# A modulation bank computed beside the keys and values, and the state-space constants cut into more steps

## The chip, the cores and the metric

The kernel runs on one core of one Trainium2 chip. The metric is the device time of one launch in microseconds, as the median of several runs. TensorE (PE) does matrix products, VectorE (DVE), ScalarE (ACT) and GpSimd (POOL) do the elementwise work, and the queue of SyncE (SP) issues almost all DMAs. Each engine takes its instructions in the order in which the program lists them.

## The reference, cut to what matters

Two layers work on 1152 tokens (1024 latent, 128 context) of width 1024. Layer 0 is windowed attention and a squared-ReLU MLP, layer 1 a state-space mixer (S5) with a GLU and a second MLP. Every block is modulated by vectors that come from a small product with a large weight.

```python
def _modulation(cvec, w_mod, b_mod):
    return jnp.split(jax.nn.silu(cvec) @ w_mod + b_mod, N_MOD, axis=-1)
...
    dt = jnp.exp(log_dt.astype(jnp.float32))[:, None]
    mag = jnp.exp(lam_re * dt)
    ang = lam_im * dt
    ab_re = mag * jnp.cos(ang)
    ab_im = mag * jnp.sin(ang)
...
for i in range(DEPTH):
    sh1, sc1, g1, sh2, sc2, g2 = _modulation(c, w_mod[i], b_mod[i])
    h = _modulate(x, norm1_g[i], sh1, sc1)
    x = x + g1 * mixer(h)            # attention in layer 0, S5 in layer 1
    x = x + g2 * _mlp(_modulate(x, norm2_g[i], sh2, sc2), mlp_w1[i], mlp_w2[i])
```

The S5 mixer needs per-group constants (exponentials, sines, cosines and complex powers of the transition) that depend on weights alone.

## The kernel before, in words

Tokens stand in three chunks of 384 columns. Most products are taken in three passes of a split operand (high by high, low by high, high by low), one matmul per pass, at L45, L46 and L47. The written program is not the final order: a scheduler places instructions on each engine by their place in the code, by priorities and by what they need; from then on each engine keeps that order.

**Start and prologue.** `start` computes modulation bank 0 of layer 0. `attention` then normalizes the chunks in the order 1, 2, 0 and computes keys (`k_part`, PSUM tiles `kps`) and values (`v_part`, `vps`) for each, and at chunk 0 the first two query tiles (`q_items`, `qps`, then `q_put`). The query weights `wq` share two buffers with the key weights `wk`.

**A modulation bank.** `mod_bank(..., ahead=True)` has eight steps. A step multiplies the 1 MB of weights of one k-tile (two tiles `wm` of 512 KB, in the two buffers with tag `wo`) into a PSUM tile `modps` (L163), and only then issues the loads of the next k-tile on SP (L145). In layer 0, two steps share one PSUM tile from a pool of two buffers (tag `st`, which `nps`, `nrb` and `qps` use as well); the sum goes to `modsb`, and four transposes (`modpt`, L178) turn it. The matmuls carry a high priority and are placed no earlier than the last product recorded before them. A generator yields after each step, so that a caller can spread the steps.

**Attention.** 72 units (24 pairs of heads in three blocks each) go through scores (`sps`, L369), softmax on DVE, ACT and POOL, transposes (`tps`), and the product with V (`pvps`). During the first 12 units `modfill` feeds banks 1 and 2 in between (20 yields); from unit 12 on the output projection (`wops`) fills that place. `wops` takes its weights through the `wo` buffers too, and its result needs the gate from bank 1.

**First MLP with the S5 preparation beside it.** `mlp(0, background)` runs 16 blocks of hidden columns. In a block PE does six tiles of the first product (24 matmuls each, called first-layer tiles here), then 24 tiles of the second (6 matmuls each), whose results DVE adds to `x` (L470); PSUM holds six such tiles. `fill` takes 2 steps of the generator `background` after each chunk of the first product and 3 after each chunk of the second:

```python
            def fill(where):
                with self.tc.high_priority(offset=-self.LOW):
                    for _ in range((self.F0, self.F1)[where]):
                        next(gen, None)
```

`background` runs `s5_prep`: 32 small blocks, each with DVE work on the tiles `bb`, `g` and `d`, POOL work on `bm`, a small product `kp` (L1288, reads `g`, high priority) and transposes `bmt`, and every eighth block first `s5_consts`. That one is about 160 short DVE instructions in tiles `ww`, `w2`, `w3` and `pq`, with three yields: after the sines and cosines, after the division, and at the end.

Of the kernel before, what the change touches and what calls it, by code (L numbers as in the profile page):

```python
# [33 lines left out]
class Body:  # L34
# [448 lines left out]
    def attention(self):  # L483
        nc, tc, a = self.nc, self.tc, self.a
        with ExitStack() as ctx:
# [9 lines left out]
            with ExitStack() as c2:  # L495
                P = c2.enter_context(tc.tile_pool(name="pro", bufs=1, reuse_waits="tile"))
                ps = c2.enter_context(tc.tile_pool(name="props", bufs=6, space=PSUM))
                wv = [P.tile([128, 2048], F32R, name=f"wv{i}") for i in range(2)]
                hs = {1: self.h_big(self.H, "h")}
                for _ in self.norm_apply(1, 0, 0, hs[1]):  # L500
                    pass
                nc.sync.dma_start(self.x[2], a["x"][2])
                self.w_kv(1, wv)
                mk = P.tile([128, 2, 128], F32, name="mkf")
                kc = P.tile([128, 2, 128], F32, name="kc")
                nc.sync.dma_start(mk, a["mask"])
                nc.sync.dma_start(self.sink, a["sink"])
                nc.sync.dma_start(kc, a["cache_k"])
                nc.sync.dma_start(self.V[:, 9], a["cache_v"])
                for _ in self.norm_stats(2):  # L510
                    pass
                hs[2] = self.h_small("h2")
                for _ in self.norm_apply(2, 0, 0, hs[2]):
                    pass
                for _ in self.norm_stats(0):
                    pass
                for c in (1, 2, 0):
                    if c == self.CC:
                        nc.vector.tensor_copy(self.mask, mk)
                        nc.vector.tensor_copy(self.identb, self.ident)  # L520
                        nc.vector.tensor_scalar(self.nsink, self.sink, -1.0, None, op0=ALU.mult)
                        for m in range(2):
                            self.put_k(m, kc[:, m, :], 1152, 128)
                    if c == 2:
                        hs[0] = self.h_big(self.H, "h")
                        for _ in self.norm_apply(0, 0, 0, hs[0]):
                            pass
                    tab = self.rope_tab(c)
                    for m in range(2):
                        self.k_part(c, m, hs[c], self.wk, tab, ps)  # L530
                    if c == 0:
                        for t in range(2):
                            out = []
                            for _ in self.q_items(t, hs[0], out):
                                pass
                            Q[t] = self.q_put(out[0], tab)
                    for j in range(3):
                        self.v_part(c, j, hs[c], wv, ps)

            B = ctx.enter_context(tc.tile_pool(name="att2", bufs=2, reuse_waits="tile"))  # L540
            self.B = B
# [36 lines left out]
            stats = {}  # L578

            def modfill():  # L580
                for b in (1, 2):
                    yield from self.mod_bank(0, b, self.R, "wo", 2, 2, B, "modsb", 2, True)

            def pace(r, n, total):

                return (r + 1) * total // n - r * total // n

            fill = modfill()
            nfill = 20
            for i in range(NU):  # L590
                c, t, jj = units[i]
                tau = 8 * c + t
                if jj == 0:
# [5 lines left out]
                    if t == 4:  # L599
                        fill, nfill = self.wo_items(c, 0, otl[c]), 16  # L600
                    if t == 0 and c > 0:
                        fill, nfill = self.wo_items(c - 1, 1, otl[c - 1]), 16
# [462 lines left out]
    def sincos(self, x, s, c, t, z, n):  # L1065

        v = self.nc.vector
        mg = 12582912.0
        self.reduce(x, n, 4)
        v.tensor_tensor(out=z, in0=x, in1=x, op=ALU.mult)  # L1070
        v.tensor_scalar(t, z, -1.9515295891e-4, 8.3321608736e-3, op0=ALU.mult, op1=ALU.add)
        v.tensor_scalar(c, z, 2.443315711809948e-5, -1.388731625493765e-3, op0=ALU.mult, op1=ALU.add)
# [4 lines left out]
        v.scalar_tensor_tensor(out=s, in0=t, scalar=1.0, in1=x, op0=ALU.add, op1=ALU.mult)  # L1077
        v.scalar_tensor_tensor(out=c, in0=c, scalar=-0.5, in1=z, op0=ALU.add, op1=ALU.mult)
        v.tensor_scalar(c, c, 1.0, None, op0=ALU.add)

        v.tensor_scalar(t, n, 0.25, mg, op0=ALU.mult, op1=ALU.add)
        v.tensor_scalar(t, t, mg, None, op0=ALU.subtract)
# [7 lines left out]
        v.tensor_tensor(out=c, in0=c, in1=z, op=ALU.mult)  # L1090
        v.tensor_tensor(out=s, in0=s, in1=t, op=ALU.subtract)
        v.tensor_tensor(out=c, in0=c, in1=x, op=ALU.add)

    NPA = 92
    NT = 147
# [2 lines left out]
    def s5_consts(self, pa, qs):  # L1098
# [6 lines left out]
        an, tt, zz, nn = (w2[:, i] for i in range(4))  # L1105
        sn, cs = (w3[:, i] for i in range(2))
# [3 lines left out]
        s0 = self.s0[:, :, qs]  # L1110
        mag = w[:, 0, :]
        self.exp_dve(dt, dt, w[:, 1, :], w[:, 2, :], w[:, 3, :])

        v.tensor_tensor(out=an[:, 0, :], in0=li, in1=dt, op=ALU.mult)
        v.tensor_tensor(out=w[:, 4, :], in0=lr, in1=dt, op=ALU.mult)
        self.reduce(an[:, 0, :], w[:, 5, :])
        for k in range(7):
            v.tensor_scalar(an[:, k + 1, :], an[:, 0, :], 8.0 * 2.0 ** k, None, op0=ALU.mult)
        self.sincos(an, sn, cs, tt, zz, nn)
        self.exp_dve(w[:, 4, :], mag, w[:, 1, :], w[:, 2, :], w[:, 3, :])  # L1120
        t, q = an[:, 0:8, :], w2[:, 1:3, 0:8, :]
        yield
# [5 lines left out]
        for n in (1, 2, 4):  # L1128
            o = slice(n + 1, 2 * n + 1)
            b = lambda z: z[:, n:n + 1, :].to_broadcast([128, n, G])  # L1130
            self.cmul(v, pr[:, o, :], pi[:, o, :], pr[:, 1:n + 1, :], pi[:, 1:n + 1, :], b(pr), b(pi),
                      t[:, 0:n, :])

        den, rd, nr, fr, fi, t1 = (w[:, 5 + i, :] for i in range(6))
        v.tensor_tensor(out=den, in0=lr, in1=lr, op=ALU.mult)
# [35 lines left out]
        for k in range(4):  # L1171
            n = 1 << k
            m = min(n, 11 - n)
            o = f0 + n
            b = lambda z: (cs, sn)[z][:, k + 1:k + 2, :].to_broadcast([128, m, G])
            self.cmul(v, F_r[:, o:o + m, :], F_i[:, o:o + m, :], F_r[:, f0:f0 + m, :], F_i[:, f0:f0 + m, :],
                      b(0), b(1), t[:, 0:m, :])
        p0, p1 = q[:, 0, 0:2], q[:, 1, 0:2]
        self.cmul(v, p0, p1, cs[:, 5:7, :], sn[:, 5:7, :], cs[:, 3:5, :], sn[:, 3:5, :], t[:, 0:2, :])
        self.cmul(v, E_r[:, 4:6, :], E_i[:, 4:6, :], p0, p1, cs[:, 1:3, :], sn[:, 1:3, :], t[:, 0:2, :])  # L1180
# [6 lines left out]
        for z_r, z_i, n in ((F_r, F_i, f0), (E_r, E_i, e0)):  # L1187
            nc.scalar.copy(z_r[:, 0:n, :], z_r[:, 2 * n:n:-1, :])
            nc.scalar.mul(z_i[:, 0:n, :], z_i[:, 2 * n:n:-1, :], -1.0)

        zs = self.zs[:, qs]
        r8 = zs[:, :, 2]
# [27 lines left out]
    def s5_prep(self, mods):  # L1220
# [9 lines left out]
        for b in range(64 // GB):  # L1230
# [71 lines left out]
                                  bass.AP(tensor=w.tensor, offset=w.offset, ap=[list(w.ap[0]), [16, 8], [1, 128]]))  # L1302
            nc.sync.dma_start(self.ex_d[lo, gs], g[lo, :, :, 1:9, :])
            nc.sync.dma_start(self.ex_d[hi, gs], g[hi, :, :, 0:8, :])
            yield
            bt = M.tile([128, GB, 2, 128], F32, name="bt", tag="bt")
            tp = self.bank("bmt")
            for q in range(GB):
# [410 lines left out]
```

## Time and profile before

| what | value |
|---|---|
| median of 3 runs | 2742.19 us |
| lowest, highest | 2741.9, 2745.39 us |
| profiled execution, its time | 2745.59 us |
| its span, first to last instruction | 2743.5 us |
| mean granted TensorE clock | 0.977 |
| PE busy | 2570.7 us, 94% |
| DVE busy | 1972.1 us, 72% |
| ACT busy | 1220.4 us, 44% |

The profiled execution is one execution, 3.4 us above the median of the others; sums are made against it. A busy PE is counted from the start of a matmul to its modelled end, at whatever clock was granted, so a stretch at half clock looks as busy as one at full clock.

### The profile page before, as it was taken

What the parts mean: (1) busy time and instruction counts of PE and PEld (TensorE: products, weight loads), DVE (VectorE), ACT (ScalarE), POOL (GpSimd) and SP (SyncE); (2) the same over time, 40 slices, a digit from 0 to 9 for tenths busy, and PEclk for the clock granted to TensorE, in tenths of its full rate; (3) what the DMA queues carried; (4) which work ended last, traced back from release to release, by engine and by line L of the source; (5) the groups of instructions that cost most, each with busy time, mean ns of one, the idle gap of its engine ahead of it and who ended that gap; (6) DMA issues with size and microseconds to landing.
All of it is one profiled execution on the core that took longest, in us unless ns stands there. A gap on an engine that the chain in (4) does not pass through costs nothing. (4 is left out here: it accounts for less than half of the span.)

```text
span 2743.5 us, 43899 instructions
## 1 busy us (share of the span) xinstructions
PE 2570.7 (94%) x16369; PEld 2418.0 (88%) x16369; DVE 1972.1 (72%) x4609; ACT 1220.4 (44%) x2519; POOL 366.6 (13%) x492
## 2 busy tenths in 40 slices
PE   6888999999999999999999678999999999999997
PEld 4767898889998998998999666899999999999997
DVE  4845777789778777769764799555577677777677
ACT  3454666665333233323233655443455445434344
POOL 1122322220221221211210310000011001000001
PEclk8999999999999999999999899999999999999998
DMA  7253222222342343343321576433333312111212
GB/s 269 81 164 126 77 82 73 85 74 86 116 134 87 115 130 107 117 123 116 112 91 49 163 234 204 138 123 123 108 121 127 130 66 91 68 62 67 72 63 77
DMA packets 138244, 305.22 MB, mean 111 GB/s; under 512 B 14384, under 2 KB 70064, under 8 KB 136624
## 3 DMA queue, kind: packets, MB, share of 16 engines
q1 hardware_dynamic: 138032, 302.42, 33.8%
q8 instruction: 130, 2.13, 0.3%
q14 instruction: 82, 0.67, 0.1%
HBM read 247.78 MB, written 39.81 MB: 105 GB/s over the span
## 5 line engine op out<-in xcount | busy, mean ns | idle before, releaser
L45 PE MATMUL m<-at,w 128*128 128x384 f32 x1536 | 522.7, 340 | 4.2 <-DVE x L470 1.9
L470 DVE SCALAR_TENSOR_TENSOR x<-m,mod,x 128x384 f32<-128x384 f32 (+2 forms) x1024 | 486.8, 509 | 54.8 <-PE m L47 51.7
L46 PE MATMUL m<-at,w 128*128 128x384 f32 x1536 | 518.6, 338 | 0.2 <-DVE at L879 0.2
L47 PE MATMUL m<-at,w 128*128 128x384 f32 x1536 | 518.5, 338 | 0.0
L45 PEld LDWEIGHTS m<-at,w 128*128 128x128 f32 x1536 | 289.8, 189 | 12.6 <-DVE x L470 5.3
L46 PEld LDWEIGHTS m<-at,w 128*128 128x128 f32 x1536 | 289.4, 188 | 0.7 <-DVE at L879 0.5
L47 PEld LDWEIGHTS m<-at,w 128*128 128x128 f32 x1536 | 289.3, 188 | 0.6 <-issue 0.4
L51 ACT CAST w<-wr 128x1024 fp32r<-128x1024 f32 x160 | 165.8, 1046 | 259.1 <-PE m L46 194.3
L52 DVE TENSOR_TENSOR w<-wr,w 128x1024 fp32r<-128x1024 f32 x160 | 197.4, 1241 | 62.3 <-ACT w L51 55.9
L45 PE MATMUL m<-h,w 128*128 128x384 f32 x512 | 175.1, 342 | 2.3 <-ACT w L51 1.5
L47 PE MATMUL m<-h,w 128*128 128x384 f32 x512 | 174.1, 340 | 2.9 <-DVE w L52 2.7
L45 PE MATMUL m<-mh,w 128*128 128x384 f32 x512 | 176.2, 345 | 0.0
L46 PE MATMUL m<-mh,w 128*128 128x384 f32 x512 | 174.3, 341 | 0.0
L47 PE MATMUL m<-mh,w 128*128 128x384 f32 x512 | 174.2, 341 | 0.0
L46 PE MATMUL m<-h,w 128*128 128x384 f32 x512 | 173.6, 339 | 0.0
L404 POOL TENSOR_SCALAR pt<-pt,sst 128x512 f32<-128x512 f32 (+1 forms) x144 | 103.6, 732 | 304.5 <-DVE sst L402 134.8
L392 ACT ACTIVATE pt<-sps,sst 128x512 f32<-128x512 f32 (+1 forms) x144 | 89.4, 626 | 71.7 <-DVE sst L381 71.4
L784 PE MATMUL m<-hs,ws 128*128 128x384 f32 x576 | 114.4, 338 | 0.0
L697 ACT ACTIVATE r<-m 128x384 f32<-128x384 f32 x96 | 46.9, 490 | 151.5 <-PE m L47 151.3
L52 DVE TENSOR_TENSOR at<-r,at 128x384 fp32r<-128x384 f32 x96 | 55.7, 581 | 76.0 <-ACT at L51 75.8
L380 DVE TENSOR_REDUCE sst<-sps 128x1 f32<-128x512 f32 (+1 forms) x144 | 86.9, 612 | 32.1 <-PE sps L378 29.2
L369 PE MATMUL sps<-K,q 128*128 128x256 f32 (+1 forms) x544 | 96.8, 304 | 11.6 <-DMA q<-q 4.5
(372 smaller groups left out, 5953.9 us busy)
## 6 DMA issues: line engine op xcount, KB each, us to landing
wr<-in_w_dram SPq DMA_DIRECT2D x192, 512.0 KB, 3.8
wm<-in_w_mod_dram SPq DMA_DIRECT2D x80, 512.0 KB, 4.8
wr<-in_glu_dram SPq DMA_DIRECT2D x48, 512.0 KB, 3.2
wr<-in_w_qo_dram SPq DMA_DIRECT2D x24, 512.0 KB, 3.2
wr<-in_w_qo_dram SPq DMA_DIRECT2D x48, 256.0 KB, 2.6
bt<-bt_d SPq DMA_DIRECT2D x16, 768.0 KB, 5.7
dt_d<-d SPq DMA_DIRECT2D x32, 294.0 KB, 3.5
D<-dt_d SPq DMA_DIRECT2D x16, 588.0 KB, 4.7
```

The costliest lines, as they stand in the source:

```text
L45: mm(out, lh, rh, start=first, stop=False)
L46: mm(out, lh, rl, start=False, stop=False)
L47: self.mm = mm(out, ll, rh, start=False, stop=last)
L51: (ceng.copy if ceng is self.nc.scalar else ceng.tensor_copy)(h, src)
L52: seng.tensor_tensor(out=l, in0=src, in1=h, op=ALU.subtract)
L369: nc.tensor.matmul(ps[:, 128 * i0:128 * i0 + w], lhs, rhs, start=(part == 0 and i0 == 0), stop=part == 1 and n == 8)
L380: nc.vector.tensor_reduce(out=mx[:, e:e + 1], in_=ps[:, :nk], axis=AX.X, op=ALU.max)
L392: nc.scalar.activation(p[:, e, :nk], sps[e][:, :nk], AF.Exp, scale=SCALE, bias=ng[:, e:e + 1], accum_out=sm[:, e:e + 1])
L404: nc.gpsimd.tensor_scalar(p[:, e, :nk], p[:, e, :nk], rc[:, e:e + 1], 1.0, op0=ALU.mult, op1=ALU.mult)
L470: nc.vector.scalar_tensor_tensor(out=self.x[c][:, m, lo:hi], in0=ps[:, lo:hi], scalar=self.gate(layer, j, m, s), in1=self.x[c][:, m, lo:hi ...
L697: nc.scalar.activation(r, pt[:, :CW], AF.Relu)
L784: self.nc.tensor.matmul(p[:, :CW], w[i][:, x, j, :], B[i][j][y], start=f and k == 0, stop=j == 3 and k == 2, skip_group_check=True)
```

## The change

Bank 1 of layer 0 is taken out of `modfill` and becomes a generator of its own, `early`, made before the loop over the chunks and advanced by one after each key part and after the first two value parts: twelve places for its ten yields. `modfill` keeps bank 2, and its pace is set for 10 instead of 20 yields over the same 12 units. In `s5_consts` the three yields become fourteen (thirteen cuts inside the work and one at its end); the arithmetic stays the same. In `s5_prep` the yield between the stores of a block and its transposes goes, so that a block takes five steps instead of six.

```diff
+                early = self.mod_bank(0, 1, self.R, "wo", 2, 2, P, "modsb", 2, True)
                 for c in (1, 2, 0):
...
                     for m in range(2):
                         self.k_part(c, m, hs[c], self.wk, tab, ps)
+                        next(early, None)
...
                     for j in range(3):
                         self.v_part(c, j, hs[c], wv, ps)
+                        if j < 2:
+                            next(early, None)
+                for _ in early:
+                    pass
...
             def modfill():
-                for b in (1, 2):
-                    yield from self.mod_bank(0, b, self.R, "wo", 2, 2, B, "modsb", 2, True)
+                yield from self.mod_bank(0, 2, self.R, "wo", 2, 2, B, "modsb", 2, True)
...
-            nfill = 20
+            nfill = 10
...
     def sincos(self, x, s, c, t, z, n):
         self.reduce(x, n, 4)
+        yield
...
         v.tensor_scalar(c, c, 1.0, None, op0=ALU.add)
+        yield
...
         v.tensor_tensor(out=c, in0=c, in1=x, op=ALU.add)
+        yield
...
         self.exp_dve(dt, dt, w[:, 1, :], w[:, 2, :], w[:, 3, :])
+        yield
...
-        self.sincos(an, sn, cs, tt, zz, nn)
+        yield
+        yield from self.sincos(an, sn, cs, tt, zz, nn)
...
         for n in (1, 2, 4):
...
             self.cmul(v, pr[:, o, :], pi[:, o, :], pr[:, 1:n + 1, :], pi[:, 1:n + 1, :], b(pr), b(pi),
                       t[:, 0:n, :])
+            yield
...
         for k in range(4):
...
+            if k % 2:
+                yield
...
             nc.scalar.mul(z_i[:, 0:n, :], z_i[:, 2 * n:n:-1, :], -1.0)
+        yield
...
             nc.sync.dma_start(self.ex_d[hi, gs], g[hi, :, :, 0:8, :])
-            yield
             bt = M.tile([128, GB, 2, 128], F32, name="bt", tag="bt")
```

The built programs show where the scheduler puts the moved work. Three places matter.

**The end of the prologue on PE.** Before, these rows stand just ahead of the first scores: one step of bank 1 among the matmuls of the third query tile.

```order
L46 MATMUL qps<-h,wq 128x384
L47 MATMUL qps<-h,wq 128x384
L163 MATMUL modps<-wm,csil 32x512 x4
L45 MATMUL qps<-h,wq 128x384
L46 MATMUL qps<-h,wq 128x384
```

Now the last three steps of bank 1 stand at the end of the values of chunk 0, with its transposes behind them, and only then the first query tile.

```order
L45 MATMUL vps<-wv_237,h 128x256
L46 MATMUL vps<-wv_238,h 128x256
L163 MATMUL modps<-wm,csil 32x512 x4
L47 MATMUL vps<-wv_237,h 128x256
L45 MATMUL vps<-wv_237,h 128x256
L46 MATMUL vps<-wv_238,h 128x256
L47 MATMUL vps<-wv_237,h 128x256
L163 MATMUL modps<-wm,csil 32x512 x8
L178 MATMUL modpt<-ident,modsb 128x128 x4
L45 MATMUL qps<-h,wq 128x384
L46 MATMUL qps<-h,wq 128x384
```

All eight steps of bank 1 now precede the queries; the first of them stands among the transposes `nrb` of the last norm statistics of the prologue (L238), and four matmuls of V are all that stands between the sixth and the seventh.

**The first small product after the second set of constants, on PE and DVE.** Before, PE has `kp_9892` inside the second product's tile `m2_9935`:

```order
L47 MATMUL m2_9927<-at_9530,w2_9372 128x384
L45 MATMUL m2_9935<-at_9530,w2_9371 128x384
L46 MATMUL m2_9935<-at_9530,w2_9371 128x384
L1288 MATMUL kp_9892<-g_9874,bz_9780 32x128 x8
L47 MATMUL m2_9935<-at_9530,w2_9372 128x384
```

and DVE finishes `g_9874` (its last row is L1034) among the constants in `ww`, just ahead of the addition of tile `m2_9911`, which PE computes three tiles before `m2_9935`:

```order
L1032 TENSOR_TENSOR ww_9460<-pq_7303 64x16 x2
L1200 TENSOR_TENSOR ww_9460<-ww_9460 128x16
L1037 TENSOR_TENSOR ww_9460<-ww_9460 64x16 x2
L1034 SCALAR_TENSOR_TENSOR g_9874<-g_9874,t_9875 128x2x144
L1201 TENSOR_TENSOR ww_9460<-ww_9460 128x16
L470 SCALAR_TENSOR_TENSOR x1_71<-m2_9911,mod0_93,x1_71 128x384
```

Now DVE finishes the corresponding `g_10203` among the first-layer splits `at_9936` of the next block (L1040 is the same line as L1034 before),

```order
L1043 TENSOR_TENSOR ww_9582<-ww_9582 64x16
L52 TENSOR_TENSOR at_9936<-r_9992,at_9936 128x384
L1043 TENSOR_TENSOR ww_9582<-ww_9582 64x16
L1040 SCALAR_TENSOR_TENSOR g_10203<-g_10203,t_10204 128x2x144
L1216 TENSOR_TENSOR ww_9582<-ww_9582 128x16
```

and PE has the product that reads it eight tiles into that block's second product, behind the tiles that use `at_9936`:

```order
L46 MATMUL m2_10277<-at_9936,w2_9926 128x384
L47 MATMUL m2_10277<-at_9936,w2_9927 128x384
L1303 MATMUL kp_10295<-g_10203,bz_10122 32x128 x8
L163 MATMUL modps_8248<-wm_9517,csil_73 32x512 x2
L163 MATMUL modps_8248<-wm_9515,csil_73 32x512 x2
```

The distance from `g` to `kp` grows from a few second-product tiles to the rest of the first product and eight tiles.

**The third set of constants on DVE.** Before, its rows around the splits of block 8 (counting from 0) are mostly its end, mixed with the next small block's `g` and `d`:

```order
L1032 TENSOR_TENSOR ww_11672<-pq_7303 64x16
L1200 TENSOR_TENSOR ww_11672<-ww_11672 128x16
L52 TENSOR_TENSOR at_12164<-r_12190,at_12164 128x384
L1037 TENSOR_TENSOR ww_11672<-ww_11672 64x16
L1296 SCALAR_TENSOR_TENSOR ks_12053<-eye_89,dcol_90,ks_12053 64x16
```

Now nearly the whole set stands in the first product of block 8, from the exponential on:

```order
L1058 SCALAR_TENSOR_TENSOR ww_11808<-ww_11808 128x16
L52 TENSOR_TENSOR at_11847<-r_11873,at_11847 128x384
L1079 TENSOR_SCALAR w3_11807<-w2_11806 128x128
L1084 SCALAR_TENSOR_TENSOR w3_11807<-w2_11806 128x128
L1081 TENSOR_TENSOR w3_11807<-w3_11807,w2_11806 128x128
L1089 TENSOR_SCALAR w2_11806<-w2_11806 128x128
```

Counted over the whole program, the DVE instructions of `background` between the last addition to `x` of one block and the first of the next are 110, 136, 107 and 160 at blocks 1, 4, 8 and 11 before (21 to 73 elsewhere from block 2 to 13), and now 40 at block 1, 85 and 70 at blocks 4 and 5, 159 at block 8, and 87 and 122 at blocks 11 and 12.

## Rows read from the trace of the kernel before

**Rows 1.** The page: PE over the span, and the granted clock in 40 slices.

```profile
PE 2570.7 (94%) x16369; PEld 2418.0 (88%) x16369; DVE 1972.1 (72%) x4609; ACT 1220.4 (44%) x2519; POOL 366.6 (13%) x492
...
PEclk8999999999999999999999899999999999999998
```

**Rows 2.** Windows: stretch and length, busy time of each engine, granted clock, DMA.

```profile
82.60:127.00 44.40, 38.42 (x251) 36.05 (x252) 41.79 (x78) 18.52 (x34) 9.06 (x7) 1.00 0.29 92
127.00:241.25 114.25, 94.27 (x712) 66.16 (x713) 50.63 (x143) 51.69 (x140) 24.09 (x34) 0.87 0.50 156
241.25:600.00 358.75, 344.18 (x2688) 305.95 (x2687) 273.69 (x698) 233.97 (x614) 103.47 (x133) 1.00 0.25 79
```

**Rows 3.** What PE waited for from 127 to 250 us: total, times, longest.

```profile
PE modps L163 <- DMA wm<-in_w_mod_dram: 14.4, 11, 2.9
```

**Rows 4.** Timeline of PE: steps of the banks, with the idle time before each.

```profile
120.83 1.06 PE L163 MATMUL modps<-wm,csil 128*32 128x512 f32 x8 [1.35 <-ACT qf L327]
...
133.06 1.94 PE L163 MATMUL modps<-wm,csil 128*32 128x512 f32 x8 [2.85 <-DMA wm<-in_w_mod_dram]
...
162.15 1.06 PE L163 MATMUL modps<-wm,csil 128*32 128x512 f32 x8 [0.64 <-DMA wm<-in_w_mod_dram]
...
168.33 1.06 PE L163 MATMUL modps<-wm,csil 128*32 128x512 f32 x8 [0.71 <-DMA wm<-in_w_mod_dram]
...
236.88 1.93 PE L163 MATMUL modps<-wm,csil 128*32 128x512 f32 x8 [2.52 <-DMA wm<-in_w_mod_dram]
```

**Rows 5.** Windows of the bank steps alone (L163): PE and PEld busy, clock, DMA.

```profile
127.00:241.25 114.25, 20.32 (x120) 2.61 (x120) 0.87 0.50 156
```

**Rows 6.** Timeline of PE: the transposes of the prologue's last norm statistics.

```profile
82.61 0.51 PE L238 MATMUL nrb<-ident,nst 128*128 128x128 f32 x3 [1.60 <-DVE nst L235]
```

**Rows 7.** Windows of the query tiles alone: PE, PEld and ACT busy, clock, DMA.

```profile
105.25:113.13 7.88, 7.85 (x44) 7.69 (x44) 0.00 (x0) 1.00 0.55 182
```

**Rows 8.** Timeline of DVE, then of PE: a query tile's shuffle, and the first scores.

```profile
120.24 0.58 DVE L275 STREAM_SHUFFLE rt<-qf 128x384 f32<-128x384 f32 x1
...
127.01 0.65 PE L369 MATMUL sps<-K,q 128*128 128x256 f32 x4 [2.81 <-ACT q L332]
```

**Rows 9.** Windows of 10 us: PE fed, and PE between waits.

```profile
110.00:120.00 10.00, 9.48 (x65) 9.16 (x63) 9.16 (x16) 3.66 (x6) 2.89 (x2) 1.00 0.31 107
...
130.00:140.00 10.00, 7.15 (x44) 4.92 (x42) 5.24 (x17) 5.86 (x15) 1.15 (x2) 0.61 0.52 181
```

**Rows 10.** What PE waited for in the first MLP, 619 to 1530 us.

```profile
PE kp L1288 <- DVE g L1034: 11.3, 4, 4.7
PE kp L1288 <- DVE ww L1201: 5.0, 1, 5.0
PE m L45 <- DVE x L470: 1.9, 3, 0.8
```

**Rows 11.** Timeline of PE: two of the small products with the wait before.

```profile
891.44 1.08 PE L1288 MATMUL kp<-g,bz 128*32 128x128 f32 x16 [4.98 <-DVE ww L1201]
...
1283.68 1.08 PE L1288 MATMUL kp<-g,bz 128*32 128x128 f32 x16 [4.72 <-DVE g L1034]
```

**Rows 12.** Windows of whole blocks 1, 3, 4, 7, 8 and 11 of the first MLP.

```profile
674.10:731.90 57.80, 55.34 (x354) 52.44 (x353) 52.58 (x172) 22.21 (x51) 14.98 (x19) 1.00 0.33 101
788.90:844.70 55.80, 55.80 (x363) 52.64 (x361) 39.13 (x106) 15.70 (x35) 13.33 (x19) 1.00 0.46 144
844.70:909.40 64.70, 57.97 (x338) 53.95 (x334) 51.93 (x236) 21.14 (x50) 7.11 (x12) 0.95 0.29 88
...
1022.40:1077.10 54.70, 54.70 (x332) 51.98 (x329) 41.35 (x154) 14.70 (x32) 4.77 (x8) 1.00 0.33 104
1077.10:1140.20 63.10, 58.71 (x371) 54.69 (x369) 58.58 (x201) 23.26 (x57) 15.63 (x22) 0.97 0.36 112
1253.50:1315.90 62.40, 57.66 (x347) 53.98 (x345) 57.23 (x230) 21.74 (x51) 10.47 (x15) 0.95 0.33 102
```

**Rows 13.** Windows: DVE's share in the first half of block 11.

```profile
1253.50:1286.00 32.50, 27.78 (x166) 27.11 (x165) 29.54 (x152) 18.07 (x41) 4.92 (x7) 0.93 0.25 82
```

## The prediction

> **What bounds the kernel now.** The page comes first: PE is busy for 94% of the span, and the slices in which the granted clock falls are few [rows 1]. So the kernel is as long as PE's work plus PE's waits plus what it does at half clock, and a change that moves work without removing any can only win the last two. The reader is then to look for the stretches where PE waits. The windows show one: from 127.0 us (first scores) to 241.25 us (first output projection) PE is busy for 94.3 of 114.25 us at a mean clock of 0.87, while later attention has 344 of 359 us at 1.00 [rows 2]. The list of PE's waits says for what: the weights of the modulation steps, 14.4 us in 11 waits [rows 3]. The timeline shows the chain behind it: 16 steps from 120.83 to 236.88 us, 7.7 us from one to the next on average, and 6.2 us where nothing else delayed them (162.15 to 168.33) [rows 4]. A step of 1.06 us frees its two buffers only when it is done, so the rest of the 6.2 us is the loading of the next 1 MB. Two banks in a row therefore pace 116 us.
>
> The second stretch is the first MLP. PE's waits there are nearly all one kind: the small product `kp` waits for DVE, 16.3 us in 5 waits [rows 10], and the timeline shows two of them at 5.0 and 4.7 us [rows 11]. The windows of whole blocks give the full price: blocks 3 and 7, with no set of constants, take 55.8 us with 363 matmul records and 54.7 us with 332, which is 0.035 us for each record more. By that line blocks 1, 4, 8 and 11 should take 55.5, 54.9, 56.1 and 55.2 us, and take 57.8, 64.7, 63.1 and 62.4 [rows 12]. They are 2.3 + 9.8 + 7.0 + 7.2 = 26.3 us too long: some 18 us of waits, the rest half clock (0.95, 0.97 and 0.95 in these windows).
>
> **The bank beside the keys and values.** No instruction is added or removed. The first step needs a PSUM buffer that the last norm statistics of the prologue hold, so it comes at about 83 us, among their transposes [rows 6]. The chain from there cannot beat 6.2 us a step; it shares SP with two loads of query weights, and I take 6.5: seven intervals put the last step at 128.5 us. PE has too little to do meanwhile: from 82.6 to 127.0 us it is busy for 38.4 us [rows 2], of which the 72 query matmuls at 0.178 us (7.85 for 44, [rows 7]) are 12.8 and one step 1.1, so keys and values are 24.5 us against 45.5 us of chain, and the queries now stand behind the bank. The last two steps find four matmuls between them, so the clock falls: the step then costs 1.94 instead of 1.06 us [rows 4]. With the addition and the transposes, an estimated 1.5 us, the queries start at 132. The first tile's 24 matmuls take 4.3 us at full clock and I give them 6; from its end to the first scores the path was 6.8 us from the shuffle on [rows 8] and about 0.5 for the copy ahead, and PE has 43 further query matmuls (7.7 us) to put there. First scores at 146 us, 19 later than before.
>
> From there the same attention work remains with 8 steps instead of 15. Of 94.3 us busy the steps were 20.3 [rows 5], which leaves 74. The clock of 0.87 means 30 us at half clock; five slow steps (9.7 us) and perhaps 9 us of idle lie in it, so some 11 us of other work ran at half speed and would take 5.5 less: 68.5. Eight steps and the transposes are 9.1. For waits I take 4% as in later attention (14.6 of 359 us, [rows 2]) and 0.6 us at each step, as in [rows 4]: 8 us. That makes 85.5, and the point that was at 241.25 comes at 231.5: **10 us gained.** Bounds: with 6.2 us a step, no half clock in the queries and the scores at 139, and 79 us after, 23 us are gained; with 7.7 us a step as in attention, scores at 153.5, and 92 us after, 4 are lost.
>
> **The constants.** The order of the changed program decides here. Each set is about 24 us of short DVE work by the four expensive blocks: in the first 32.5 us of block 11 DVE is busy for 29.5 [rows 13]. What stalls PE is how much of it stands in one first product, where six tiles last 24 x 0.178 x 6 = 25.6 us by the rate of [rows 7], and that `kp` follows close behind. The first, second and fourth sets are spread (40; 85 and 70; 87 and 122 instructions), and block 7 before, with 73, lost nothing [rows 12]. The `kp` behind each set now stands a whole first product later than its `g`, so its wait has 25 us of cover, and would cost up to 5 us if that cover were gone [rows 11]. But the third set still stands as one: 159 instructions at block 8 against 160 at block 11 before. I keep that block's 7.2 us, and 1 us for the 122 at block 12, which is like 107 to 110 before without the `kp` behind it. **26.3 - 8.2 = 18 us gained.** Bounds: all 26.3; or 7, if block 8 costs 9.8, block 12 costs 7.2 and the two blocks with 85 and 87 cost 1 each.
>
> **At nothing.** The yield that goes from `s5_prep`, and the eleven that come, change the count of steps from 214 to 226 with the ten empty ones ahead; `fill` offers 15 x 16 = 240, so the preparation still ends under block 15's products. If it did not, its last steps would stand bare before S5, at 1 to 3 us each by the `kp` rows and their DVE work. The pace of bank 2, one step per 1.5 units, is slower than its chain.
>
> The sum: 2745.6 - 10 - 18 = 2717.6 for an execution like the profiled one. That one is 3.4 us above the median, so 2714.
>
> **A rule against the change.** First the rows: where PE is fed the clock is 1.00, and between two waits of some 2.8 us it is 0.61 over 10 us [rows 9, 4]; a step then takes 1.94 us. The Trainium skill, TensorE: Matmul & The Clock Gate, section "HAM oscillation — how this bites in real kernels", says that a loop which waits for a DMA at each tile throttles the array again at every tile, so that each burst starts slow. By this rule all seven intervals of the moved bank run at half clock, not only the last three. The trace agrees in part: in attention five of the fifteen steps after the first were slow ([rows 4] show two of them, at 133.06 and 236.88). The rival that follows from it is worked out below from rows.
>
> **The rivals.**
> (a) Half clock through the whole moved bank. PE's 24.5 us of keys and values and nine us of steps double to 67 us from 83 on; the last step ends at 150 instead of 130.5, the scores come at 165, and attention loses 9. For it: the waits at each step. Against it: clock 1.00 from 82.6 to 127.0 in spite of 6 us of idle [rows 2], and 4 to 5 us of work between the first five steps. 2745.6 + 9 - 18 - 3.4 = 2733.
> (b) The constants do not do what they are cut for: the scheduler gathers them in the first products anyway, as it visibly does at block 8, and blocks 5, 11 and 12 pay too. 7 us instead of 18: 2725.
> (c) Softmax paces attention once the steps are thinner. For it: scores wait for a copy or for ACT here and there. Against it: later attention with 4% idle. With 92 instead of 85.5 us after the scores, 2720 to 2721.
> (d) Slower than before: the chain of bank 1 is held on SP. Its loads for the sixth and seventh step stand behind a rope table and two query weights which wait for DVE, and such a hold can be long: the step at 133.06 came 12.2 us after the one at 120.83 [rows 4]. At 12.2 us for all seven intervals the last step comes at 168 instead of 128.5, and 2714 becomes 2754. It decides from 10.5 us a step on, where the 28 us are lost. Against it: DVE is done with the keys of chunk 0 by then, and only two of the seven loads stand there.
>
> **How the numbers follow.** Forecast, 2702 to 2726: 0.64. Better than that, down to 2692 (both upper bounds nearly met): 0.09. (a) 0.07, (b) or (c) at their far ends, 2726 to 2737: 0.13. (d) and what else would be slower: 0.07. The range of 2698 to 2734 leaves out about a tenth on either side. A change within 0.2% (5.5 us), about what a measurement of this kernel tells from none, is 2737 to 2748: 0.07, the upper ends of (a) and of the bounds. Slower 0.06, faster 0.87.
>
> **What would show it.** Right: first scores near 146 us, steps of bank 1 6 to 7 us apart with the last near 128; the first output projection near 225 to 232, with few half-clock stretches between; no `kp` wait over 1 us in the first MLP; blocks 1, 4 and 11 at 55 to 57 us, and block 8 some 7 us too long with DVE busy throughout. Wrong: a clock under 0.8 from 90 to 120 us (a); blocks 5 and 12 over 58 us (b); a gap over 9 us between steps of bank 1 (d); or a first MLP that is as long as before.

## The result, and the profile after

The changed kernel takes 2699.83 us (median of 4 runs, 2698.64 to 2705.88) against 2743.79 for the kernel before (4 runs): ratio 0.9844, 95% interval 0.9827 to 0.9862. Run again beside other kernels it took 2706.85 against 2743.22, ratio 0.9869 (0.9855 to 0.9884). So it is 36 to 44 us faster. The profiled execution, at 2705.88 us (span 2704.1), is the slowest of the first four; against the profile of before (span 2743.5) it is 39.4 us shorter. The forecast was 2714.

Where the 39.4 us lie is read from windows over the same work on both sides. First the kernel before, its rows for everything up to the first MLP, the first MLP up to the first state-space matmul, and the rest:

```profile
0.00:619.30 619.30, 548.80 (x4047) 464.26 (x4047) 426.67 (x1058) 347.43 (x873) 145.45 (x182) 0.96 0.35 115
...
619.30:1542.90 923.60, 894.67 (x5514) 848.21 (x5515) 690.16 (x2116) 309.62 (x675) 154.81 (x231) 0.99 0.34 106
...
1542.90:2743.50 1200.60, 1127.23 (x6810) 1105.50 (x6810) 855.27 (x1436) 563.35 (x973) 66.31 (x80) 0.98 0.34 113
```

and the changed kernel:

```profile
0.00:607.10 607.10, 542.39 (x4048) 460.66 (x4048) 426.48 (x1058) 345.90 (x873) 145.47 (x182) 0.96 0.35 117
...
607.10:1508.00 900.90, 885.73 (x5513) 847.68 (x5513) 689.79 (x2116) 309.35 (x675) 158.61 (x231) 0.99 0.35 109
...
1508.00:2704.10 1196.10, 1125.35 (x6810) 1103.00 (x6810) 855.09 (x1436) 563.16 (x973) 66.12 (x80) 0.98 0.34 114
```

The counts agree within one record, so no work is gone. Attention with its prologue is 12.2 us shorter: 5.8 of waits (the length less PE's busy time, 70.5 and 64.7 us) and 6.4 of less busy time for the same matmuls, most of it work that no longer runs at half clock: from the first scores to the first output projection the mean clock is 0.98 (below) against 0.87 in [rows 2]. The first MLP is 22.7 us shorter, 13.8 of it waits and 8.9 busy time. The rest is 4.5 us shorter though nothing in it changed. Of the thirteen profiles of this document, twelve have 1195 to 1202 us from the first state-space matmul to the end, and the thirteenth, with the step put back, 1189, so I count these 4.5 us as scatter.

The timeline of PE in the changed kernel shows the moved bank, the first query, the first scores and the first output projection (columns as in [rows 4]):

```profile
83.19 1.07 PE L163 MATMUL modps<-wm,csil 128*32 128x512 f32 x8
89.50 1.07 PE L163 MATMUL modps<-wm,csil 128*32 128x512 f32 x8 [0.93 <-DMA wm<-in_w_mod_dram]
...
108.66 1.06 PE L163 MATMUL modps<-wm,csil 128*32 128x512 f32 x8 [0.74 <-DMA wm<-in_w_mod_dram]
117.15 1.06 PE L163 MATMUL modps<-wm,csil 128*32 128x512 f32 x8 [1.65 <-DMA wm<-in_w_mod_dram]
...
124.49 1.93 PE L163 MATMUL modps<-wm,csil 128*32 128x512 f32 x8 [5.61 <-DMA wm<-in_w_mod_dram]
131.69 1.93 PE L163 MATMUL modps<-wm,csil 128*32 128x512 f32 x8 [5.27 <-DMA wm<-in_w_mod_dram]
...
135.23 0.67 PE L45 MATMUL qps<-h,wq 128*128 128x384 f32 x1
...
149.61 0.65 PE L369 MATMUL sps<-K,q 128*128 128x256 f32 x4
...
224.17 0.45 PE L45 MATMUL wops<-ot,wo 128*128 128x384 f32 x1
```

The windows of the last part of the prologue and from the first scores to the first projection:

```profile
82.60:133.60 51.00, 34.57 (x235) 24.49 (x235) 34.23 (x70) 14.05 (x27) 6.23 (x5) 0.90 0.57 186
149.60:224.17 74.57, 70.08 (x598) 54.20 (x598) 47.51 (x132) 46.36 (x127) 23.74 (x32) 0.98 0.46 146
```

The scores begin 22.6 us later than in [rows 8], and the output projection 17.1 us earlier than before. Not all of the 17.1 is gained, because the scheduler has moved the projection ahead of some of attention's work. The windows of the probability products alone, from the first projection to the end of attention, show it, before and after:

```profile
241.25:619.30 378.05, 59.46 (x772) 42.24 (x772) 16.29 (x57) 15.06 (x57) 1.00 0.26 82
```

```profile
224.17:607.10 382.93, 61.52 (x806) 43.71 (x804) 17.18 (x60) 15.80 (x60) 1.00 0.25 80
```

34 more of them follow, and the stretch is 4.9 us longer; 17.1 - 4.9 are the 12.2 us.

In the first MLP the small product no longer appears among PE's waits ([rows 10] had 16.3 us of it):

```profile
PE m L45 <- DVE x L470: 4.2, 3, 2.7
PE m L47 <- DVE w L52: 2.1, 2, 1.2
PE m L45 <- ACT w L51: 0.5, 1, 0.5
```

The windows of blocks 1, 3, 5, 8 and 12, of the first product of block 1, and of block 8 in its two products, show what is left:

```profile
1049.50:1075.40 25.90, 25.90 (x152) 25.82 (x149) 23.16 (x143) 14.70 (x33) 0.72 (x2) 1.00 0.32 97
1075.40:1107.40 32.00, 28.64 (x146) 27.84 (x146) 28.41 (x78) 3.53 (x7) 3.89 (x5) 0.89 0.17 53
...
662.60:687.90 25.30, 25.30 (x145) 25.30 (x145) 9.15 (x41) 11.98 (x24) 0.00 (x0) 1.00 0.12 42
...
662.60:714.00 51.40, 51.40 (x306) 50.95 (x305) 34.20 (x126) 19.53 (x39) 4.16 (x6) 1.00 0.13 44
771.20:828.10 56.90, 56.90 (x376) 53.40 (x372) 42.62 (x104) 17.40 (x41) 13.46 (x21) 1.00 0.46 147
881.40:935.30 53.90, 53.90 (x338) 52.21 (x336) 44.20 (x135) 17.21 (x36) 9.12 (x13) 1.00 0.28 90
1049.50:1107.40 57.90, 54.55 (x297) 53.67 (x294) 51.57 (x220) 18.23 (x40) 4.60 (x6) 0.94 0.24 73
1275.90:1330.00 54.10, 53.29 (x318) 51.49 (x318) 48.25 (x177) 20.00 (x45) 8.20 (x12) 1.00 0.27 85
```

The prediction's line (54.7 us for 332 records, 0.035 for each) does not hold for these blocks: it gives block 1 with its 306 records 53.8 us, and PE, which never waits there, needs 51.4. Between blocks 1 and 3, neither with a wait, a record costs 0.079 us. By that line block 8 should take 50.7 us with its 297 records and takes 57.9: about 7 us too long, nearly all of it in the second product (32.0 us against 26.1 in block 1), where PE waits 3.4 us for the additions to `x` that DVE reaches late and then runs in part at half clock (0.89). In four other profiles with the same sets it takes 55.8 to 56.8 us. Block 12 has 0.8 us of waits.

The distance behind the third set of constants, from DVE's last row of `g` to the first `kp`, is 33.8 us:

```profile
1081.61 0.46 DVE L1040 SCALAR_TENSOR_TENSOR g<-g,t 128x288 f32<-128x288 f32 x1
...
1115.89 0.65 PE L1303 MATMUL kp<-g,bz 128*32 128x128 f32 x16
```

Behind the second and the fourth set it is 18.4 and 21.3 us, behind the first 1.0. In the kernel before the first `kp` behind each set started 0.1 us after its `g`.

### The profile page after: what moved, and what is told of

It reads as the page before. It is cut to its first block, busy times and chain, and to the rows that moved or that the text cites. A ratio compares the mean times of both kernels' runs of the same rounds, so it can differ in the third digit from the quotient of the medians.

```text
span 2704.1 us, 43884 instructions
## 1 busy us (share of the span) xinstructions
PE 2553.5 (94%) x16369; PEld 2411.3 (89%) x16369; DVE 1971.4 (73%) x4609; ACT 1218.4 (45%) x2519; POOL 370.2 (14%) x492
## 5 line engine op out<-in xcount | busy, mean ns | idle before, releaser
L955 DVE TENSOR_TENSOR r<-r,m 128x384 f32<-128x384 f32 x48 | 26.5, 552 | 108.9 <-PE m L790 108.9
```

The lines of the kernel that those rows point to most:

```text
L955: add = nc.vector.tensor_tensor(out=z[i], in0=z[i], in1=p[:, :CW], op=ALU.add)
```

## Experiments

Ratios are to the kernel before, run in turn on the same chip.

**The bank alone.** The kernel before with the hunks in `attention` only.

```diff
+                early = self.mod_bank(0, 1, self.R, "wo", 2, 2, P, "modsb", 2, True)
...
-            nfill = 20
+            nfill = 10
```

> The kernel before with the moved bank alone: bank 1 of the first layer's modulation beside the keys and values, constants in three steps and the preparation in six steps as before. Theory (the two parts act each in its own stage and add up): attention as in the changed kernel, that is first scores at about 149 us instead of 127 and the first MLP from 607 instead of 619 us, and the first MLP as before with waits of 4 to 5 us of the small product for DVE; 10 to 14 us faster than before, 2730 to 2734. Rival (what attention gained is chance, since half of the 12 us are half-clock stretches that fall otherwise from run to run): 3 to 7 us, 2737 to 2741.

2731.23 us, ratio 0.9959 (0.9942 to 0.9975): 11.7 us faster by the medians. The first MLP starts at 607.5 us, as in the changed kernel, and its blocks are as long as before. The gain in attention is no chance.

**The constants' part alone.** The kernel before with the hunks in `sincos`, `s5_consts` and `s5_prep` only, for example

```diff
         self.reduce(x, n, 4)
+        yield
```

> The kernel before with the other part alone: constants in fourteen steps and the preparation in five, bank 1 in attention as before. Theory (the parts add up; the profiled first MLP fell from 923.6 to 900.9 us): first MLP of about 901 us, no wait of the small product above 1 us, one long block (the ninth, index 8); 22 to 30 us faster than before, 2714 to 2722. Rival (the first MLP gains only in company with the moved bank, which leaves another clock or another load order behind): 10 to 16 us faster, 2728 to 2734.

2719.5 us, ratio 0.9913 (0.9896 to 0.993): 23.4 us faster, and blocks 0 to 14 take 832.6 us against 833.8 in the changed kernel and 857.6 before. The theory holds. Together the two parts give 35.1 us.

**The changed kernel again**, unedited, because 35.1 is not 44.0.

> The changed kernel once more, unedited, beside the other kernels of this call: the two parts alone gave 11.7 and 23.4 us, 35.1 together, and the whole change 44.0, in runs that did not stand side by side. Theory (the parts add up and the 8.9 us between are the scatter of the runs): 2704 to 2710 here. Rival (the two parts gain 9 us more together than apart): 2697 to 2702.

2706.85 us, 36.4 below the kernel before: the parts add up, and I take the larger figure for scatter (the two intervals, 0.9827 to 0.9862 and 0.9855 to 0.9884, overlap).

**The removed step put back.**

```diff
             nc.sync.dma_start(self.ex_d[hi, gs], g[hi, :, :, 0:8, :])
+            yield
             bt = M.tile([128, GB, 2, 128], F32, name="bt", tag="bt")
```

> The changed kernel with the removed step of the preparation put back: six steps for each of 32 pieces instead of five, so 258 steps in all against 240 that the first MLP draws. Theory (the removal costs nothing only because 226 steps fit into 240): eighteen steps, three pieces of the preparation, stand bare between the first MLP and the state-space stage, at 1 to 3 us each as the prediction has it; 18 to 54 us slower than the changed kernel, 2718 to 2754. Rival (they hide under the last norm statistics and the first loads of the state-space stage): within 5 us of the changed kernel, 2695 to 2705.

2749.24 us, ratio 1.0028 (1.0015 to 1.004): slower than the kernel before, so the whole gain is gone. The timeline of PE behind the first MLP shows three pieces of the preparation one engine at a time, POOL, DVE and PE waiting for each other:

```profile
1510.41 1.08 PE L1303 MATMUL kp<-g,bz 128*32 128x128 f32 x16 [2.48 <-DVE g L1040]
1517.43 0.47 PE L1325 MATMUL bmt<-ident,bm 128*128 128x128 f32 x1 [5.94 <-POOL bm L1273]
...
1524.69 1.08 PE L1303 MATMUL kp<-g,bz 128*32 128x128 f32 x16 [4.01 <-DVE g L1040]
...
1535.48 1.08 PE L1303 MATMUL kp<-g,bz 128*32 128x128 f32 x16 [3.65 <-DVE g L1040]
1541.93 0.47 PE L1325 MATMUL bmt<-ident,bm 128*128 128x128 f32 x1 [5.36 <-POOL bm L1273]
...
1555.59 4.13 PE L1398 MATMUL V<-u,bt 128*64 128x145 f32 x32 [11.26 <-DMA u<-hs]
```

The first state-space matmul comes at 1555.6 instead of 1508.0 us: 47.6 us for 18 steps that find no place, 2.6 each, near the upper end of the 1 to 3 that the prediction named. In the first MLP itself, where the sets now fall at other places, no `kp` is among PE's waits, as in the changed kernel:

```profile
PE m L45 <- DVE x L470: 8.4, 6, 3.0
PE m L47 <- DVE w L52: 2.5, 2, 1.3
```

**Nothing cut, the distance kept.** Each set is issued whole in its first step, and the thirteen steps behind are empty.

```diff
-                yield from self.s5_consts(pq, slice(GB * b, GB * b + self.GQ))
+                n = sum(1 for _ in self.s5_consts(pq, slice(GB * b, GB * b + self.GQ)))
+                for _ in range(n):
+                    yield
```

> The changed kernel with each set of constants issued as a whole in its first step and the thirteen other steps left empty, so that the small product stands as far behind its set as in the changed kernel but nothing is cut. Theory of the prediction (how much DVE work stands in one first product stalls PE, and cutting spreads it): three more blocks 5 to 7 us too long, like the ninth, so 15 to 21 us slower than the changed kernel, 2715 to 2721. Rival (the cut does nothing by itself, since the scheduler orders short DVE work by its own clock; what helped is that the products for which the set's work is wanted come later): within 5 us of the changed kernel, 2695 to 2705, with one long block, the ninth, as there.

2707.75 us, ratio 0.9877 (0.9856 to 0.9899), against 0.9869 for the changed kernel (0.9844 in its first runs). The 15 to 21 us of the theory are excluded, and the rival holds. The windows of blocks 1, 8 and 12 of this kernel, and of the first product of block 1:

```profile
666.00:691.30 25.30, 25.30 (x146) 25.30 (x145) 23.76 (x108) 15.12 (x33) 4.40 (x6) 1.00 0.18 55
...
666.00:717.40 51.40, 51.40 (x307) 50.95 (x305) 42.92 (x146) 19.08 (x39) 4.40 (x6) 1.00 0.17 54
...
1052.90:1109.80 56.90, 53.37 (x297) 52.60 (x294) 51.13 (x220) 18.27 (x40) 4.56 (x6) 0.97 0.24 74
1278.40:1333.20 54.80, 53.26 (x318) 51.45 (x317) 47.59 (x168) 19.92 (x45) 7.76 (x12) 1.00 0.26 84
```

Block 1 carries 8.7 us more DVE work than in the changed kernel (42.92 against 34.20), its first product 23.76 against 9.15, and is no longer; block 8 is long again. In blocks 8 and 12 DVE is as busy as with the cut (51.13 and 51.57, 47.59 and 48.25 us): there the scheduler spread the uncut sets by itself, so only the first set tests uncut work in one product. Block 0, where that set begins, takes 58.2 us against 55.5 in the changed kernel and 54.2 to 56.6 in other kernels that cut it, so up to some 3 us for the cut are not excluded.

**Only the step removed**, in the kernel before: sets in three steps, the preparation in five. That makes 182 steps (10 + 4 x 3 + 32 x 5), not the 202 of the expectation.

```diff
             nc.sync.dma_start(self.ex_d[hi, gs], g[hi, :, :, 0:8, :])
-            yield
             bt = M.tile([128, GB, 2, 128], F32, name="bt", tag="bt")
```

> The kernel before with only the one step of the preparation removed (202 steps): sets in three steps, the small product one step nearer to its operand than before. Theory (the gain of the constants' part is the thirteen steps between a set and its first small product, not the step removed): the waits of the small product remain, 4 to 7 us at three or four places, and the time stays within 8 us of the kernel before, 2735 to 2747. Rival (the removed step is what helped, by putting the sets elsewhere): 15 us or more faster, 2728 or less.

2739.71 us, ratio 0.9989 (0.998 to 0.9997), and PE's waits in the first MLP are those of before:

```profile
PE kp L1288 <- DVE g L1034: 11.9, 5, 5.0
PE kp L1288 <- DVE ww L1032: 3.4, 1, 3.4
```

So what helps is neither the cut nor the step removed. It is the steps, full or empty, that stand between a set and the first small product that reads it: with three of them `kp` waits wherever the sets fall (the kernel before, this one), with fourteen or more it does not, cut or uncut, at the three places that the runs gave the sets (the changed kernel, the step put back, and the shifted sets that follow).

**The sets shifted.** Six empty steps behind the second and the third set in the changed kernel move the third and fourth to the place in their blocks that the second has; 238 steps of 240 are used.

```diff
                 yield from self.s5_consts(pq, slice(GB * b, GB * b + self.GQ))
+                for _ in range((0, 6, 6, 0)[b // 8]):
+                    yield
```

> The changed kernel with six empty steps behind the second and behind the third set of constants, so that the third and fourth set fall at the same place in their blocks as the second does: 238 steps, still under 240. Theory (the ninth block is long because 32.4 us of DVE work are queued in its first product of 25.9 us; the order then has no block with more DVE work than its product lasts): no block above 57.5 us, the first MLP 4 to 6 us shorter, 3 to 7 us faster than the changed kernel. Rival (the long block follows the set wherever it falls): no difference beyond 2 us.

2703.86 us, ratio 0.9859 (0.9842 to 0.9876): 3.0 us below the changed kernel measured beside it, within the intervals. The window of block 8 shows what the time alone would not: no wait, clock 1.00.

```profile
1048.60:1102.00 53.40, 53.40 (x325) 52.09 (x322) 41.98 (x186) 17.85 (x42) 4.57 (x7) 1.00 0.33 106
```

The 32.4 us of the expectation was a sum of durations that overlap: in the changed kernel DVE is busy for 23.2 of the 25.9 us of that product. The six steps also lengthen the distance behind the second and third set, but no `kp` waited there before. From its start to the first state-space matmul the first MLP takes 893.4 us, against 898.6 in the changed kernel's second run.

**Shifted and uncut**, both edits together.

```diff
-                yield from self.s5_consts(pq, slice(GB * b, GB * b + self.GQ))
+                n = sum(1 for _ in self.s5_consts(pq, slice(GB * b, GB * b + self.GQ)))
+                for _ in range(n):
+                    yield
+                for _ in range((0, 6, 6, 0)[b // 8]):
+                    yield
```

> The shifted sets of e6, each issued as a whole in its first step with the others empty. Theory after e4 (the steps work as distance between a set and the first small product that needs it, and the place of the set in its block decides the rest; the cut inside the set does nothing): within 4 us of e6, 2700 to 2708, and no long block except perhaps block 1, whose first product gets the whole first set. Rival of the prediction (the cut spreads the work): 8 us or more slower than e6, 2712 or more.

2702.52 us, ratio 0.9859 (0.9842 to 0.9876), the same as cut.

**An earlier bank.** The accumulator of the moved bank gets a PSUM buffer of its own, taken from the prologue's six, and its first load is issued ahead of the norm statistics of chunk 2.

```diff
-            ps = self.bank("modps")
+            ps = psum.tile([128, 512], F32, name="modps", tag="modps", bufs=1) if psum else self.bank("modps")
...
-                ps = c2.enter_context(tc.tile_pool(name="props", bufs=6, space=PSUM))
+                ps = c2.enter_context(tc.tile_pool(name="props", bufs=5, space=PSUM))
+                mps = c2.enter_context(tc.tile_pool(name="modps", bufs=1, space=PSUM))
...
+                early = self.mod_bank(0, 1, self.R, "wo", 2, 2, P, "modsb", 2, True, psum=mps)
+                next(early)
                 mk = P.tile([128, 2, 128], F32, name="mkf")
```

> The changed kernel with the moved bank 1 given a PSUM buffer of its own (the prologue's accumulators go from six to five) and its generator started before the norm statistics of chunk 2, so that its steps need not wait for the last norm statistics at 83 us. Theory (the prologue after the change is held by the bank's chain of loads from 83.2 to 133.6 us, 25 us of idle PE; begun some 25 us earlier the chain ends among the keys and values): steps from 55 to 60 us on, first scores at 130 to 138 us instead of 149.6, 10 to 18 us faster than the changed kernel. Rival (the weights of the bank then meet those of the keys and values and x on the DMA queues, and steps come 10 us apart): within 5 us of the changed kernel.

2691.04 us, ratio 0.9811 (0.9797 to 0.9826): 15.8 us below the changed kernel. The first MLP starts at 590.7 us instead of 607.1. PE's timeline:

```profile
59.67 1.75 PE L163 MATMUL modps<-wm,csil 128*32 128x512 f32 x8
...
83.00 1.06 PE L163 MATMUL modps<-wm,csil 128*32 128x512 f32 x8
...
108.66 1.07 PE L163 MATMUL modps<-wm,csil 128*32 128x512 f32 x8 [1.05 <-DMA wm<-in_w_mod_dram]
...
131.62 0.65 PE L369 MATMUL sps<-K,q 128*128 128x256 f32 x4 [3.86 <-DMA q<-q]
```

The chain is no faster (49 us for seven intervals), but it ends at 109.7 among the keys and values, and the scores start at 131.6, now behind the DMA of a query tile (3.9 us of wait). The buffer and the earlier place were not tried apart.

**Two steps' weights on their way**, from the four buffers with tag `ot`, which attention uses later and the prologue for the normalized chunk 2. The place in the program is that of the change.

```diff
-                if ahead and kt < KT - 1:
+                if two:
+                    ws, nx = nx, load(kt + 2) if kt < KT - 2 else None
+                elif ahead and kt < KT - 1:
                     ws = load(kt + 1)
```

> The changed kernel with four buffers for the weights of the moved bank, taken from those that attention uses later, so that two steps' weights are on their way at a time; its start at 83 us stays. Theory (each of the seven intervals of 6.2 to 8.5 us is free buffer, issue, 4 to 5 us of landing, step, so PE waits for one load latency per step, 16 us in all): intervals of 3.5 to 5 us where the order of the keys and values allows them, the last step 8 to 14 us earlier than 133.6, and 6 to 12 us faster than the changed kernel. Rival (not latency but what the queues can carry, or the place of the steps in PE's order, sets the pace): within 3 us of the changed kernel, 2703 to 2709.

2696.64 us, ratio 0.9841 (0.9824 to 0.9858), 7.7 us below the changed kernel's 0.9869 by the ratios, though the intervals touch, and no better than the 0.9844 of its first runs. The time alone does not settle it. The timeline shows the intervals shrink, the last step come 10.7 us earlier though the first came 9.6 later, and the scores start at 144.6 us; the first MLP starts at 596.8 instead of 607.1.

```profile
SPq L145 <- PE vps L47: 21.0, 4, 20.1
...
92.84 1.07 PE L164 MATMUL modps<-wm,csil 128*32 128x512 f32 x8 [0.24 <-DMA wm<-in_w_mod_dram]
96.31 1.07 PE L164 MATMUL modps<-wm,csil 128*32 128x512 f32 x8
100.30 1.07 PE L164 MATMUL modps<-wm,csil 128*32 128x512 f32 x8 [0.44 <-DMA wm<-in_w_mod_dram]
...
121.00 1.55 PE L164 MATMUL modps<-wm,csil 128*32 128x512 f32 x8 [4.48 <-DMA wm<-in_w_mod_dram]
...
144.60 0.57 PE L372 MATMUL sps<-K,q 128*128 128x256 f32 x4
```

The first row, from the waits of SP between 55 and 90 us, gives the reason for the late start: SP waits 20.1 us for value products, which read chunk 2 in the `ot` buffers, and issues the bank's first loads at 85.7 us, where the changed kernel issued them at 46.1.

**Early bank and shifted sets together**, the edits of those two kernels.

```diff
+                early = self.mod_bank(0, 1, self.R, "wo", 2, 2, P, "modsb", 2, True, psum=mps)
...
+                for _ in range((0, 6, 6, 0)[b // 8]):
+                    yield
```

> The early bank with its own PSUM buffer and the shifted sets together. Theory (each works in its own stage, 15.8 and 3.0 us below the changed kernel): 2685 to 2690, faster than every kernel so far. Rival (the earlier bank takes the clock or the loads that the shift gains by): 2690 to 2694.

2687.43 us, ratio 0.9805 (0.979 to 0.9821): the fastest of all by the median, 17.6 us below the changed kernel's 0.9869 by the ratios. Against the early bank alone (0.9811) the shift cannot be told from nothing.

## Why the prediction was right, and where not

**The bank** went as forecast, and the size was near: 10 us forecast, 12.2 measured in the profiles, 11.7 alone. The first step came at 83.2 us, the intervals were 6.2 to 8.5 us (6.9 on average, 6.5 forecast), the last step at 131.7 instead of 128.5, the scores at 149.6 instead of 146. The term that was mis-sized is what follows: 85.5 us from the scores to the projection. It took 74.6, or 79.5 with the work that changed places, 6.0 less than forecast. The 8 us put for waits were 3.5 too many, since PE was busy for 70.1 of the 74.6; the rest is busy time. That the total came within 2.2 us is partly luck, since scores 3.6 us late and a following stretch 6.0 us short nearly cancel. The bound with 7.7 us a step puts the scores at 153.5; added up like the forecast it is 154.4. That the chain of loads is what the moved bank costs, and not the half clock or PE's work, two experiments show: begun 23.5 us earlier, it lets the scores start 18 us earlier, and with two loads ahead the intervals are 2.4 to 5.6 us.

**Half clock through the moved bank** (a) did not come. First the rows: the six steps up to 117.15 us took 1.06 to 1.07 us, five of them behind waits of 0.7 to 1.7 us, and only the last two, behind 5.6 and 5.3 us of wait, took 1.93. That is the 1.94 that the prediction gave them, but its four matmuls stand ahead of the first of the two, and none of V stands between them. The Trainium skill, TensorE: Matmul & The Clock Gate, section "HAM oscillation — how this bites in real kernels", tells of a loop whose matmuls take less time than its wait for the next load, and has the array throttled again at every tile there. The prediction left that condition out. With it this trace agrees on both sides: the first six steps had 4.3 to 5.8 us of other matmuls between them against waits of 0.7 to 1.7, the last two under 1 us against more than 5.

**SP holding the chain** (d) was wrong: the longest interval was 8.5 us, and 10.5 was the point from which it would decide. **Softmax as the pace** (c) was wrong: PE waited for 4.5 of the 74.6 us behind the first scores.

**The constants** gained 22.7 us in the profile against 18. The residue in that profile is as forecast: about 7 us at block 8 (7.2 forecast) and 0.8 us of waits at block 12 (1 forecast). What was too small is the 26.3 us from which it was taken. By 0.079 instead of 0.035 us for each record, from 51.4 us at 306, the four long blocks of before were 27.8 us too long; that is 1.5 of the missing 4.7 us, and the others I cannot place. The same line is why block 1, at 51.4 us, lies below the 55 to 57 that were named for it. The small product waits nowhere, as forecast, but its cover was not the same 25 us behind each set: 1.0, 18.4, 33.8 and 21.3 us. (b) is wrong, since blocks 5 and 12 took 53.9 and 54.1 us. But one step of the reasoning failed. The prediction counted the instructions of a set in one first product, and took the smaller counts at blocks 1, 4, 5 and 11 to be the source of the gain. Issued uncut, the first set stands in block 1 with 42.9 us of DVE work and costs nothing there, and the time is the same in both pairs (0.9877 and 0.9869; 0.9859 twice). What the changed kernel wins is the other half of that paragraph: the small product comes far enough behind its operand. The place of a set still decides at block 8, where shifting took the long block away, but of that 3 to 5 us reach the whole, not 18; and the busy share of DVE does not tell such a block, since blocks 8 and 12 of the changed kernel both have 0.89, with 3.4 and 0.8 us of waits.

**At nothing.** The removed step did cost nothing, for the reason given, and the margin is 14 steps. With the step kept there are 258 for 240 places, and the change would have been a loss.

**The sum** was 2714 where the first runs gave 2699.8 and the second 2706.9. Of the 11.4 us between the profile's 39.4 and the forecast's 28, the attention is 2.2, the first MLP 4.7, and 4.5 the scatter of the unchanged rest.

Open: a cut without the distance could not be made, as every cut is also a step, so that it does nothing (within some 3 us) is shown only with the distance there.

## What to carry to other kernels

A generator that is drawn step by step sets two things, how finely work is dealt out and how far a consumer stands behind its producer; try empty steps before cutting work, and count that all steps find a place, since those left over stand bare on the path. Work whose loads are a chain belongs where other work lasts as long as the chain, and it must be able to start there: here a shared PSUM buffer and a late place in the order, which of the two was not tried apart, held it back by 23.5 us, and cost 15.8 us where the move itself had gained 11.7.

## What the runs showed of the hardware

With weights for two steps on their way the queues gave much more than the chain had used. The windows of the changed kernel and of that one over their first five steps (the last two columns are the DMA share and GB/s):

```profile
83.20:108.70 25.50, 21.98 (x156) 17.48 (x158) 22.51 (x46) 11.27 (x21) 3.88 (x3) 1.00 0.61 201
```

```profile
92.80:113.00 20.20, 18.98 (x130) 13.79 (x130) 11.70 (x22) 6.13 (x10) 2.40 (x2) 1.00 0.87 299
```

299 GB/s at a DMA share of 0.87, other loads included, against 201 and 0.61. At that rate 1 MB takes 3.5 us, which is the interval between the first two steps: so, as an estimate from these figures, about half of the 6 to 8 us of the chain was waiting for one load at a time, and 3.5 us are about what the queues gave here.
